# A tuned four-layer decoder trunk: the RMSNorm's per-token scale is spread over the partitions by two passes of ones on diagonal tiles in place of four, and later in the FFN

## The chip, the cores and the metric

The kernel runs on one core of a Trainium2 chip, as one program. The metric is the device time of one execution in microseconds (us). The engines are TensorE (PE, the matmuls, with a queue of its own for weight loads, PEld), VectorE (DVE), ScalarE (ACT), GpSimd (POOL) and SyncE (SP, which issues the weight transfers).

## What is computed

Four layers on 256 tokens of 1024 features. Each layer is a first gated feed-forward network (FFN), a token mixer, a second FFN, and a gated addition of an embedding (PLE). Every one of these four begins with an RMSNorm, so there are 16 norms.

```python
def rmsnorm(x, gain):
    xf = x.astype(jnp.float32)
    y = xf * lax.rsqrt(jnp.mean(xf * xf, axis=-1, keepdims=True) + EPS)
    return (y * gain.astype(jnp.float32)).astype(x.dtype)

def swiglu(x, w_gu, w_down):
    g, u = jnp.split(x @ w_gu, 2, axis=-1)
    return (jax.nn.silu(g) * u) @ w_down
# each layer:
#  h = x + 1/2 * SwiGLU_1(RMSNorm(x))
#  h = h + Mixer_{i mod 3}(RMSNorm(h))      (0 HGRN2, 1 mLSTM, 2 sliding window)
#  h = h + 1/2 * SwiGLU_2(RMSNorm(h))
#  x = h + sigmoid(RMSNorm(h) W_gate) * (p[i] W_ple)
```

## The kernel before, in words

All activations lie transposed: features on the 128 partitions, 256 tokens along the row. `h[0]` to `h[3]` hold the residual stream, each two feature tiles of 256 columns. Products are made to fp32 accuracy from fp32r parts: a number is split into a high and a low part, and three of the four partial products are summed.

**Weights** stream through in units of 1024 columns (`unit`, L225 is the transfer). Each unit is split: ACT casts the high part (`wh`, L250), DVE subtracts it from the raw weight (`wl`, L251). Six `wh` tiles and six `wl` tiles are in rotation, so a cast has to wait until PE has finished with the unit six before. `mm_t` then makes two matmuls for a 128x128 piece of weight: L282 (128x512: high weight with the high and the low part of x) and L283 (128x256: low weight with the high part of x). The first four columns of a product are made with the feature tile in the outer loop, so that a product can begin when the first x tile is there. L272 to L274 are the three matmuls of the form without folding.

**The norm is delayed.** The products do not wait for it: `push_tile` multiplies h by the gain only (L254 on ACT for the high part, L255 on DVE for the low part of an x tile, 128x256 each), and the product's result is multiplied by 1/rms afterwards. Meanwhile `norm_steps` makes 1/rms beside the product: squares, sums, a matmul with ones that gives each token's sum in a column (L416), a multiply-add (L390, DVE), a power of -0.5 (L391, POOL), which leaves `rc` with the tokens on the partitions. Then the spread turns `rc` into `rb`, where each partition holds all 256 values: for each half of the tokens a fp32 matmul of `rc` (broadcast along the row) with the identity (L421), which the chip runs as two passes each, four in all; ACT copies the result out (L423). These steps are background work of the product: `tick` counts units of weights, and a step is emitted when the weight of its predecessor (`yield W_RC`) has passed. The framework's scheduler then sets the final order on each engine, which runs its instructions in that order.

**Who reads rb.** In the FFN L442 (DVE) before the Silu; in HGRN L689. In PLE, `add`: the accumulators are folded (L311 on ACT, L312 on DVE) into `gs`, multiplied by rb (L544, DVE), a sigmoid follows (L545, ACT), two products (L546, L547, DVE) give the new h, and `push_tile` makes the next layer's x tiles from it. The next layer's first FFN product therefore begins behind PLE's whole chain.

**HGRN** multiplies gate slabs pairwise on DVE (L730, with the reciprocals L736 and L738) and makes the level matmuls L723 and, for the widest levels, L711 with `kc`, in two groups of four heads; PE has weight products in between. L808 scales the accumulators by rc.

Of the kernel before, what the change touches and what calls it, by code (L numbers as in the profile page):

```python
# [10 lines left out]
F32 = mybir.dt.float32  # L11
F32R = mybir.dt.float32r
# [6 lines left out]
P = 128  # L19
D = 1024  # L20
T = 256
NT = T // P
# [5 lines left out]
EPS = 1e-6  # L28
U = 1024
AHEAD_UNITS = 3  # L30
W_SQ, W_SS, W_RC = 1.0, 0.5, 0.5
ML_RATE = 1
SW_RATE = 2.5
FQ_RATE = 0.75
# [24 lines left out]
def weight_plan():  # L59
# [34 lines left out]
    for l, kind in enumerate(kinds()):  # L94
        j = (l // 3,)
        ffn(l, 0)
        if kind == 0:
            for hg in range(2):
                tiles("hg_w_in", j, run(D + hg * 512, 4) + run(hg * 512, 4), KT, 4)
            full("hg_w_in", j, 2 * D)  # L100
            for hf in range(2):
                pairs("hg_w_in", j, 3 * D + hf * 512, range(KT))
        elif kind == 1:
            tiles("ml_w_qkvo", j, run(0, 8), KT, 4)
            full("ml_w_qkvo", j, D)
            for hf in range(2):
                pairs("ml_w_qkvo", j, 2 * D + hf * 512, range(KT))
        else:
            pairs("sw_w_qkv", j, D, range(KT))
            for g in range(SW_H // SW_G):  # L110
                for k0 in (0, 4):
                    plan.append([("sw_w_qkv", j, k, [(g * 256, 256)]) for k in range(k0, k0 + 4)])
        full("w_ple_proj", (l,), 0, PLE // P)
        by_k(("hg_w_out", "ml_w_out", "sw_w_o")[kind], j)
        ffn(l, 1)
        tiles("w_ple_gate", (l,), run(0, KT), KT, 4)
# [3 lines left out]
class Kern:  # L120
# [30 lines left out]
    def small(self, shape, tag, bufs=2, dtype=F32):  # L151
        return self.tmp.tile(shape, dtype, tag=tag, name=self.nm(tag), bufs=bufs)

    def s512(self, name):
        return self.tmp.tile([P, 512], F32, tag="s512", name=self.nm(name), bufs=7)

    def pair(self):

# [190 lines left out]
    def setup(self):  # L349
        nc, c, a = self.nc, self.const, self.a  # L350
        self.h = [c.tile([P, 512], F32, tag=f"h{j}", name=f"h{j}") for j in range(4)]
        self.gains = c.tile([P, DEPTH * N_GAIN * KT], F32, name="gains")
        nc.scalar.dma_start(out=self.gains, in_=a["gains"])
        ncol = a["cols"].shape[1]
        self.cols = c.tile([P, ncol], F32, name="cols")
        self.ident = c.tile([P, P], F32, name="ident")
        make_identity(nc, self.ident)
        self.ones = c.tile([P, 1], F32, name="ones")
        nc.gpsimd.memset(self.ones, 1.0)
        self.mhalf = c.tile([P, 16], F32, name="mhalf")  # L360
        nc.gpsimd.memset(self.mhalf, -0.5)

# [27 lines left out]
        nc.vector.tensor_scalar(out=out, in0=src, scalar1=1.0 / n, scalar2=EPS, op0=ALU.mult, op1=ALU.add)  # L390
        nc.gpsimd.tensor_tensor(out=out, in0=out, in1=self.mhalf[:, :w], op=ALU.pow)  # L391

    def end_norm(self):


        rc = self.small([P, NT], "rc", 2)
        rb = self.small([P, T], "rb", 2)
        return self.x, rc, rb, self.later(self.norm_steps(rc, rb))

    def norm_steps(self, rc, rb):  # L400
        nc = self.nc
        ss = self.small([P, T], "ss", 2)
        for j in range(4):
            sq = self.s512("sq")
            nc.scalar.activation(sq, self.h[j], AF.Square)
            for i in range(2):
                s = sq[:, i * T:(i + 1) * T]
                if i:
                    nc.vector.tensor_tensor(out=ss, in0=ss if j else sq[:, :T], in1=s, op=ALU.add)
                elif j:  # L410
                    nc.vector.tensor_tensor(out=ss, in0=ss, in1=s, op=ALU.add)
            yield W_SQ
        yield W_SS
        ps = self.misc()
        for t in range(NT):
            nc.tensor.matmul(ps[:, t:t + 1], ss[:, t * P:(t + 1) * P], self.ones, start=True, stop=True)  # L416
        self.rsqrt_mean(rc, ps[:, :NT], D, NT)
        yield W_RC
        pb = self.misc()
        for t in range(NT):  # L420
            nc.tensor.matmul(pb[:, t * P:(t + 1) * P], rc[:, t:t + 1].broadcast_to([P, P]), self.ident,  # L421
                             start=True, stop=True)
        nc.scalar.copy(out=rb, in_=pb[:, :T])  # L423

    @staticmethod
# [7 lines left out]

    def ffn(self, l, f):
        nc = self.nc
        x, rc, rb, norm = self.end_norm()
        aT = [None] * FT
        todo = deque()

        def gate(j, g, u):  # L440

            nc.vector.tensor_tensor(out=self.two(g), in0=self.two(g), in1=self.bc(rb), op=ALU.mult)  # L442
            nc.scalar.activation(g, g, AF.Silu)  # L443
            nc.vector.tensor_tensor(out=g, in0=g, in1=u, op=ALU.mult)  # L444
            s = self.wide(F32R) if j >= 9 else self.slab(F32R)
            s4 = s.rearrange("p (c h t) -> p c h t", c=2, h=2)
            self.split(s4[:, :, 0, :], s4[:, :, 1, :], self.two(g))
            for i in range(2):
                aT[2 * j + i] = s[:, i * 512:(i + 1) * 512]

        def flush():
            while todo:
                gate(*todo.popleft())

        def gated(c, ps):
            if c % 2 == 0:
                return
            j = c // 4
            t = self.fold(ps, self.s512("gu"))
            if c % 4 == 1:  # L460
                self.g = t
                return
            todo.append((j, self.g, t))
            if len(todo) > 1:
                self.settle(norm)
            if norm not in self.bg:
                flush()

        self.gemm_tiles(x, 2 * FT, 4, gated)
        self.settle(norm)  # L470
        flush()
        self.start_norm(self.gain(l, 2 * f + 1))

        def added(c, ps):
            if c % 2 == 0:
                return
            j = c // 2
            y = self.fold(ps, self.s512("y"))
            nc.vector.tensor_tensor(out=self.two(y), in0=self.two(y), in1=self.bc(rb), op=ALU.mult)
            nc.vector.scalar_tensor_tensor(out=self.h[j], in0=y, scalar=0.5, in1=self.h[j],  # L480
                                           op0=ALU.mult, op1=ALU.add)
            self.push(j)

        self.gemm_tiles(aT, KT, 2, added)
# [800 lines left out]
```

## Time and profile before

| what | value |
|---|---|
| median of 3 runs | 2116.18 us (2113.44 to 2116.35) |
| the profiled execution's own time | 2116.68 us |
| its span in the trace | 2114.8 us |
| PE busy | 2087.5 us, 99% |
| PE weight loads busy | 1823.5 us, 86% |
| DVE busy | 1540.9 us, 73% |
| ACT busy | 1205.7 us, 57% |
| POOL busy | 52.9 us, 2% |

Busy times are sums over the whole execution. Matmuls are pipelined, so PE's busy time runs from a start to a modelled end; what a matmul costs PE is read from the distance between two starts. PE does not wait much, so the reader should look for the few places where it does.

### The profile page before, as it was taken

The page shows a single profiled execution, that of the slowest core. Times are in us where ns is not written, and L with a number is a line of the kernel's source. Part 1 is how long each engine was busy: PE and PEld are TensorE (multiplying, and loading weights), DVE is VectorE, ACT ScalarE, POOL GpSimd, SP SyncE. Part 2 cuts the span into 40 slices and gives each one's busy share as a digit, 9 for nine tenths or more (in the row PEclk, how much of TensorE's full clock was granted, in tenths as well). Part 3 has the DMA queues.
Part 4 walks back from the last instruction along what each step waited for, and adds up shares of the span by engine and source line. Part 5 has one row for each costly group of instructions (what it writes and reads, how often), then busy time and mean ns, then how long its engine had stood idle before and what let it go on. Part 6 is the DMA issues. An engine that isn't in the chain of part 4 may idle for free.

```text
span 2114.8 us, 30580 instructions
## 1 busy us (share of the span) xinstructions
PE 2087.5 (99%) x12269; PEld 1823.5 (86%) x12269; DVE 1540.9 (73%) x2065; ACT 1205.7 (57%) x1678; POOL 52.9 (2%) x84
## 2 busy tenths in 40 slices
PE   8999999999999999999999999999999999999998
PEld 7888889888888888888888888788888888898887
DVE  7766987776877576776687667777687768967766
ACT  6554656554755466655565557655465545565554
POOL 2000000000000000000000001000000000000000
PEclk9999999999999999999999999999999999999999
DMA  7555344555455544555555552355545453355552
GB/s 277 201 191 180 116 164 165 199 188 190 167 197 195 188 163 154 181 197 184 194 179 182 196 179 101 120 186 192 189 170 199 180 185 134 141 179 180 198 182 78
DMA packets 53999, 372.26 MB, mean 176 GB/s; under 512 B 6368, under 2 KB 7136, under 8 KB 9568
## 3 DMA queue, kind: packets, MB, share of 16 engines
q1 hardware_dynamic: 53712, 370.24, 48.8%
q8 instruction: 96, 1.57, 0.3%
q14 instruction: 47, 0.39, 0.1%
q10 hardware_dynamic: 144, 0.07, 0.0%
HBM read 369.23 MB, written 1.05 MB: 175 GB/s over the span
## 4 chain that ended last, share of the span: by engine, by line
PE 91%; DVE 4%; issue 2%; ACT 1%; POOL 1%; DMA 0%; SPq 0%; DVEq 0%; ACTq 0%; POOLq 0%
PE acc L282 50%; PE acc L283 25%; PE acc L272 2%; PE acc L274 2%; PE acc L273 2%; PE acc L264 2%; PE acc L263 2%; PE acc L265 2%; PE mis L723 1%; DVE wl L251 1%; DVE slab L730 1%; PE mis L1106 1%; DVE slab L736 1%; POOL rc L391 0%; PE mis L421 0%
## 5 line engine op out<-in xcount | busy, mean ns | idle before, releaser
L282 PE MATMUL acc<-x,wh 128*128 128x512 f32 x3384 | 1186.4, 395 | 6.0 <-ACT wh L250 5.9
L251 DVE TENSOR_TENSOR wl<-wraw,wh 128x1024 fp32r<-128x1024 f32 (+1 forms) x693 | 845.1, 1222 | 473.3 <-ACT wh L250 469.5
L250 ACT CAST wh<-wraw 128x1024 fp32r<-128x1024 f32 (+1 forms) x693 | 726.6, 1050 | 745.5 <-PE acc L282 434.6
L283 PE MATMUL acc<-x,wl 128*128 128x256 f32 x3384 | 947.3, 280 | 0.0
L282 PEld LDWEIGHTS acc<-x,wh 128*128 128x128 f32 x3384 | 635.8, 188 | 153.2 <-ACT wh L250 5.9
L283 PEld LDWEIGHTS acc<-x,wl 128*128 128x128 f32 x3384 | 639.1, 189 | 0.4 <-DVE wl L251 0.4
L282 PE MATMUL acc<-slab,wh 128*128 128x512 f32 x1152 | 403.8, 394 | 0.0
L283 PE MATMUL acc<-slab,wl 128*128 128x256 f32 x1152 | 321.5, 279 | 0.0
L282 PEld LDWEIGHTS acc<-slab,wh 128*128 128x128 f32 x1152 | 215.9, 187 | 50.0
L283 PEld LDWEIGHTS acc<-slab,wl 128*128 128x128 f32 x1152 | 217.2, 189 | 0.0
L312 DVE TENSOR_TENSOR gu<-acc,gu 128x512 f32<-128x512 f32 x176 | 120.4, 684 | 7.5 <-ACT gu L311 6.9
L311 ACT COPY gu<-acc 128x512 f32<-128x512 f32 x176 | 102.0, 580 | 16.9 <-PE acc L283 16.8
L272 PE MATMUL acc<-wh,x 128*128 128x512 f32 (+1 forms) x272 | 103.1, 380 | 0.0
L273 PE MATMUL acc<-wl,x 128*128 128x512 f32 (+1 forms) x272 | 100.8, 371 | 0.0
L274 PE MATMUL acc<-wh,x 128*128 128x512 f32 (+1 forms) x272 | 100.7, 370 | 0.0
L282 PE MATMUL acc<-wide,wh 128*128 128x512 f32 x256 | 91.7, 394 | 0.0
L263 PE MATMUL acc<-slab,wh 128*128 128x256 f32 x256 | 74.1, 291 | 0.1
L264 PE MATMUL acc<-slab,wh 128*128 128x256 f32 x256 | 72.9, 285 | 0.0
L265 PE MATMUL acc<-slab,wl 128*128 128x256 f32 x256 | 72.6, 284 | 0.0
L283 PE MATMUL acc<-wide,wl 128*128 128x256 f32 x256 | 71.4, 279 | 0.0
L254 ACT ACTIVATE x<-h,gains 128x256 fp32r<-128x256 f32 x128 | 57.5, 502 | 20.4 <-DVE h L480 19.9
L444 DVE TENSOR_TENSOR gu<-gu,gu 128x512 f32<-128x512 f32 x88 | 60.8, 692 | 6.0 <-ACT gu L443 2.9
(246 smaller groups left out, 1791.8 us busy)
## 6 DMA issues: line engine op xcount, KB each, us to landing
wraw<-in_w_all SPq DMA_DIRECT2D x346, 1024.0 KB, 4.8
wraw<-in_w_all SPq DMA_DIRECT2D x7, 512.0 KB, 7.8
pt<-in_pT SPq DMA_DIRECT2D x4, 256.0 KB, 4.1
h<-in_xT SPq DMA_DIRECT2D x3, 256.0 KB, 6.2
outT<-h SPq DMA_DIRECT2D x3, 256.0 KB, 2.0
wraw<-in_w_all SPq DMA_DIRECT2D x2, 256.0 KB, 4.5
h<-in_xT SPq DMA_DIRECT2D x2, 128.0 KB, 3.2
outT<-h SPq DMA_DIRECT2D x1, 128.0 KB, 1.7
```

The source lines that it names most:

```text
L250: self.nc.scalar.copy(out=hi, in_=src)
L251: self.nc.vector.tensor_tensor(out=lo, in0=src, in1=hi.bitcast(F32), op=ALU.subtract)
L263: mm(ps, wh[:, cs], xh, start=first and opens, stop=False, skip_group_check=True)
L264: mm(ps, wh[:, cs], xl, start=False, stop=False, skip_group_check=True)
L265: mm(ps, wl[:, cs], xh, start=False, stop=last, skip_group_check=True)
L272: mm(ps, xh[:, ts], wh[:, cs], start=first, stop=False, skip_group_check=True)
L273: mm(ps, xh[:, ts], wl[:, cs], start=False, stop=False, skip_group_check=True)
L274: mm(ps, xl[:, ts], wh[:, cs], start=False, stop=last, skip_group_check=True)
L282: mm(ps, wh[:, cs], x, start=first, stop=False, skip_group_check=True)
L283: mm(ps[:, T:], wl[:, cs], x[:, :T], start=False, stop=last, skip_group_check=True)
L311: nc.scalar.copy(out=o3, in_=p4[:, :, 1, :])
L312: nc.vector.tensor_tensor(out=o3, in0=p4[:, :, 0, :], in1=o3, op=ALU.add)
```

## The change

Three edits. A constant `ones_r` of 128x128 ones in fp32r is added. Behind `rc`, `split_scaled` makes two diagonal tiles of 128x128 for each of the high and the low part (identity times rc), which is two ACT (L254) and two DVE (L255) instructions of 128x128 per norm; the spread is then two fp32r passes of 128x256, ones times the high diagonals and ones times the low ones. And the FFN norms wait for 1.25 units in place of 0.5 between rc and the spread.

```diff
-W_SQ, W_SS, W_RC = 1.0, 0.5, 0.5
+W_SQ, W_SS, W_RC, W_RC_FFN = 1.0, 0.5, 0.5, 1.25
...
-    def s512(self, name):
-        return self.tmp.tile([P, 512], F32, tag="s512", name=self.nm(name), bufs=7)
+    def s512(self, name, dtype=F32):
+        return self.tmp.tile([P, 512], dtype, tag="s512", name=self.nm(name), bufs=7)
...
+        self.ones_r = c.tile([P, P], F32R, name="ones_r")
+        nc.scalar.copy(out=self.ones_r, in_=self.ones.broadcast_to([P, P]))
...
-    def end_norm(self):
+    def end_norm(self, w_rc=W_RC):
...
-        return self.x, rc, rb, self.later(self.norm_steps(rc, rb))
-
-    def norm_steps(self, rc, rb):
+        return self.x, rc, rb, self.later(self.norm_steps(rc, rb, w_rc))
+
+    def norm_steps(self, rc, rb, w_rc):
...
         self.rsqrt_mean(rc, ps[:, :NT], D, NT)
-        yield W_RC
+
+        d = self.s512("diag", F32R)
+        dh, dl = d[:, :T], d[:, T:]
+        for t in range(NT):
+            ts = slice(t * P, (t + 1) * P)
+            self.split_scaled(dh[:, ts], dl[:, ts], self.ident, rc[:, t:t + 1])
+        yield w_rc
         pb = self.misc()
-        for t in range(NT):
-            nc.tensor.matmul(pb[:, t * P:(t + 1) * P], rc[:, t:t + 1].broadcast_to([P, P]), self.ident,
-                             start=True, stop=True)
+        for i, d in enumerate((dh, dl)):
+            nc.tensor.matmul(pb[:, :T], self.ones_r, d, start=i == 0, stop=i == 1)
         nc.scalar.copy(out=rb, in_=pb[:, :T])
...
     def ffn(self, l, f):
         nc = self.nc
-        x, rc, rb, norm = self.end_norm()
+        x, rc, rb, norm = self.end_norm(W_RC_FFN)
```

From `end_norm` on the lines of the changed kernel stand some 7 further down: L421 and L423 become L429 and L430, L545 becomes L552, L723 becomes L730. The edits also move instructions that they do not touch, as the scheduler orders anew. Three places follow; numbers behind a name are the program's own and differ between the two kernels.

ACT in the PLE of layer 0, from the spread to the first x tiles of layer 1's FFN (x_4978 before, x_5000 in the change). Before:

```order
L250 CAST wh_5024<-wraw_5022 128x1024
L423 COPY rb_4810<-mis_4953 128x256
L545 ACT_TABLE_LOAD
L545 ACTIVATE gs_4909<-gs_4909 128x512
L311 COPY gs_4971<-acc_4923 128x512
L545 ACTIVATE gs_4916<-gs_4916 128x512
L250 CAST wh_5058<-wraw_5022 128x1024
L250 CAST wh_5086<-wraw_5084 128x1024
L254 ACTIVATE x_4978<-h_82,gains 128x256 x2
```

The change, at the same place (wh_5080 is the unit that was wh_5058, wh_5108 that which was wh_5086; acc_5027 is PLE's last accumulator):

```order
L254 ACTIVATE diag_4956<-ident,rc_4826 128x128 x2
L250 CAST wh_5080<-wraw_5044 128x1024
L430 COPY rb_4827<-mis_4975 128x256
L311 COPY gs_4993<-acc_4940 128x512
L250 CAST wh_5108<-wraw_5106 128x1024
L552 ACT_TABLE_LOAD
L552 ACTIVATE gs_4926<-gs_4926 128x512
L552 ACTIVATE gs_4933<-gs_4933 128x512
L552 ACTIVATE gs_4993<-gs_4993 128x512
L311 COPY gs_5066<-acc_5027 128x512
L250 CAST wh_5132<-wraw_5106 128x1024
L254 ACTIVATE x_5000<-h_82,gains 128x256 x2
```

The rb copy now has a cast ahead of it, and all three sigmoids, two folding copies and two casts stand between it and the first x tile, where a table load, two sigmoids, one copy and two casts stood.

PE in the first FFN product of layer 1, where the spread stands. Before, with the reduction L416 ahead of it:

```order
L416 MATMUL mis_5181<-ones,ss_5065 128x1 x2
L283 MATMUL acc_5170<-x_4987,wl_5111 128x256
L282 MATMUL acc_5170<-x_4996,wh_5110 128x512
L283 MATMUL acc_5170<-x_4996,wl_5111 128x256
L282 MATMUL acc_5170<-x_4996,wh_5110 128x512
L283 MATMUL acc_5170<-x_4996,wl_5111 128x256
L421 MATMUL mis_5200<-ident,rc_5056 128x128 x2
L282 MATMUL acc_5170<-x_5051,wh_5110 128x512
```

The change, the end of the same accumulator (its reduction stands 20 matmuls ahead of the first pass):

```order
L282 MATMUL acc_5192<-x_5073,wh_5132 128x512
L283 MATMUL acc_5192<-x_5073,wl_5133 128x256
L429 MATMUL mis_5239<-diag_5208,ones_r 128x256
L282 MATMUL acc_5192<-x_5073,wh_5132 128x512
L283 MATMUL acc_5192<-x_5073,wl_5133 128x256
L429 MATMUL mis_5239<-diag_5208,ones_r 128x256
L282 MATMUL acc_5252<-x_5000,wh_5158 128x512
```

The spread has moved from 5 matmuls behind the reduction to 20, and a pair of product matmuls stands between its two passes.

PE in the HGRN mixer of layer 0, second group of heads, at the first level matmul (L723; L730 in the change). Before:

```order
L274 MATMUL acc_2365<-wh_2427,x_1708 128x512
L272 MATMUL acc_2365<-wh_2427,x_1708 128x512
L273 MATMUL acc_2365<-wl_2428,x_1708 128x512
L274 MATMUL acc_2365<-wh_2427,x_1708 128x512
L723 MATMUL mis_2415<-slab_2068,slab_2350 128x128 x4
L723 MATMUL mis_2421<-slab_2068,slab_2350 128x128 x4
```

The change (wh_2439 is the unit that was wh_2427):

```order
L274 MATMUL acc_2377<-wh_2402,x_1715 128x512
L272 MATMUL acc_2376<-wh_2439,x_1715 128x512
L272 MATMUL acc_2377<-wh_2439,x_1715 128x512
L272 MATMUL acc_2615<-wh_2528,x_1463 128x512
L730 MATMUL mis_2427<-slab_2080,slab_2362 128x128 x4
L730 MATMUL mis_2433<-slab_2080,slab_2362 128x128 x4
```

The level matmuls stood behind all twelve matmuls of that unit and now stand behind two of them and one of a later unit.

## Rows read from the trace of the kernel before

**Rows 1.** The page: span, busy times, chain by engine, one group of weight loads.

```profile
span 2114.8 us, 30580 instructions
PE 2087.5 (99%) x12269; PEld 1823.5 (86%) x12269; DVE 1540.9 (73%) x2065; ACT 1205.7 (57%) x1678; POOL 52.9 (2%) x84
...
PE 91%; DVE 4%; issue 2%; ACT 1%; POOL 1%; DMA 0%; SPq 0%; DVEq 0%; ACTq 0%; POOLq 0%
...
L282 PEld LDWEIGHTS acc<-x,wh 128*128 128x128 f32 x3384 | 635.8, 188 | 153.2 <-ACT wh L250 5.9
```

**Rows 2.** One line, L421: durations in ns, idle before it.

```profile
L421 PE MATMUL mis<-ident,rc x64: 270/275/376, 41.9 to 2100.2; 128*128 128x128 f32 x64
...
  POOL rc L391: 12.0, 18
```

**Rows 3.** Timeline, layer 1's first FFN product: start us, us, instruction, idle before.

```profile
571.30 1.61 POOL L391 TENSOR_TENSOR rc<-rc,mhalf 128x2 f32<-128x2 f32 x1 [24.54 <-DVE rc L390]
...
571.60 0.28 PE L283 MATMUL acc<-x,wl 128*128 128x256 f32 x1
...
572.96 0.71 PE L421 MATMUL mis<-ident,rc 128*128 128x128 f32 x4 [1.08 <-POOL rc L391]
...
573.43 0.47 PE L282 MATMUL acc<-x,wh 128*128 128x512 f32 x1
```

**Rows 4.** PE's timeline, layer 0's PLE: the spread, and the last and first products.

```profile
546.81 0.71 PE L421 MATMUL mis<-ident,rc 128*128 128x128 f32 x4
547.28 0.36 PE L283 MATMUL acc<-x,wl 128*128 128x256 f32 x1
...
554.77 0.40 PE L282 MATMUL acc<-x,wh 128*128 128x512 f32 x1
555.01 0.28 PE L283 MATMUL acc<-x,wl 128*128 128x256 f32 x1
555.12 0.39 PE L282 MATMUL acc<-x,wh 128*128 128x512 f32 x1
```

**Rows 5.** ACT's timeline in the same stretch.

```profile
546.16 1.05 ACT L250 CAST wh<-wraw 128x1024 fp32r<-128x1024 f32 x1 [1.69 <-issue]
547.56 0.37 ACT L423 COPY rb<-mis 128x256 f32<-128x256 f32 x1 [0.35 <-PE mis L421]
547.95 1.28 ACT L545 ACT_TABLE_LOAD   x1
549.25 0.63 ACT L545 ACTIVATE gs<-gs 128x512 f32<-128x512 f32 x1
549.83 0.59 ACT L311 COPY gs<-acc 128x512 f32<-128x512 f32 x1
...
552.48 1.05 ACT L250 CAST wh<-wraw 128x1024 fp32r<-128x1024 f32 x1 [0.59 <-ACT wh L250]
553.43 0.91 ACT L254 ACTIVATE x<-h,gains 128x256 fp32r<-128x256 f32 x2
```

**Rows 6.** DVE's timeline in the same stretch.

```profile
553.97 0.89 DVE L255 SCALAR_TENSOR_TENSOR x<-h,gains,x 128x256 fp32r<-128x256 f32 x2 [0.36 <-ACT x L254]
```

**Rows 7.** Windows: stretch, length, busy time of the engines, granted clock (PEclk), DMA.

```profile
229.10:234.30 5.20, 3.77 (x28) 3.31 (x27) 5.20 (x9) 0.79 (x1) 0.00 (x0) 1.00 0.00 0
1266.20:1268.40 2.20, 0.00 (x0) 0.00 (x0) 1.02 (x3) 1.03 (x3) 0.47 (x1) 1.00 0.00 0
1268.40:1271.80 3.40, 3.40 (x16) 3.40 (x17) 1.52 (x2) 3.40 (x8) 0.00 (x0) 0.50 0.17 19
```

**Rows 8.** Timeline of PE and DVE in the HGRN mixer of layer 0.

```profile
230.92 0.46 PE L723 MATMUL mis<-slab,slab 128*128 128x128 f32 x2 [1.43 <-DVE slab L730]
...
253.70 0.49 PE L711 MATMUL mis<-slab,kc 128*128 128x128 f32 x2 [0.46 <-ACT kc L708]
...
264.21 3.35 DVE L736 RECIPROCAL slab<-slab 128x512 f32<-128x512 f32 x1
...
272.87 1.35 PE L723 MATMUL mis<-slab,slab 128*128 128x128 f32 x10 [0.95 <-DVE slab L730]
```

## The prediction

> **What bounds the kernel now.** I read the page first: busy times, then the chain that ended last. TensorE (PE) is busy 2087.5 of 2114.8 us and holds 91% of the chain; ScalarE (ACT) and VectorE (DVE) have 57% and 73% [rows 1]. So an edit pays only where PE waits or in PE's own passes, and it costs only where an engine with slack in the mean has none in one place. PE's pace comes from its timeline: in the PLE product a wide matmul takes its slot for .24 us and a narrow one for .11 us, start to start (554.77, 555.01, 555.12) [rows 4]; I use .35 us for the pair and .117 for the narrow one. Whatever a stretch takes above that pace is loss.
>
> Next came the line that is edited. The old spread has 64 passes, four for each of 16 norms, and the profile puts 12.0 us of idle time in front of them down to POOL's power (18 times, since PE's matmul and weight-load sequencers are both counted) [rows 2]. The timeline shows that this idle time is uneven. In a PLE norm the four passes take the place of one narrow slot for .47 us (546.81 to 547.28) and nothing waits long [rows 4]. In the first FFN half of layers 1 to 3, POOL's power takes 1.61 us and PE stands: the last narrow matmul starts at 571.60, its slot ends at 571.72, and the next product starts at 573.43, so 1.71 us are lost [rows 3]. Then I read ACT's and DVE's timelines from the PLE spread to the first product of the next FFN, since the PLE result, through ACT and DVE, is the only place where the spread feeds PE directly [rows 5, 6].
>
> **The change, part by part.**
>
> *Fewer passes.* 16 norms, two passes fewer each: .47 us becomes two narrow slots, .23 us, so .24 us each where nothing waits. The new pass is 128x256 in fp32r, as the narrow product is, and I price it like that one (.117); the bound above is the .18 us that an old pass takes when four take .71 [rows 4], which would add .06 x 32 = 2 us.
>
> *The diagonal tiles.* Each norm gains two ACT and two DVE instructions of 128x128. Not in the trace; on ACT between half of a 128x256 scaled copy and a whole one (.23 to .46, from .91 for two [rows 5]), and I take .35, so .70 for two, since part of a short instruction does not shrink with its size; on DVE between half of a 128x256 scale-and-subtract and a whole one (.22 to .45, from .89 for two [rows 6]), and I take .3. On engines with 43% and 27% idle that is nothing in the mean, and it is priced below where something queues behind it.
>
> *Later spread in the FFN.* In layers 1 to 3, first half, the spread moves from 5 matmuls (.9 us) behind the reduction to 20 (3.5 us). 1.61 us of power and the diagonal tiles (.7 and .3) fit in that, with .9 left for the reduction and the multiply-add. The 1.71 us fall to the passes' .23 and some .15 of splitting: -1.3 x 3 = **-3.9**. The four second halves had no long wait: -.25 x 4 = **-1.0**. What reads rb in the FFN (L442, behind the fold that frees the accumulator) is needed by the down product alone, far later; a late rb costs nothing there.
>
> *The PLE handover, where the cost is.* The PLE's delay weight is unchanged, yet the printed order of ACT moves there, in layers 0, 1 and 2 alike. Before: cast, rb copy, table load, sigmoid, copy, sigmoid, two casts, first new x tile. After: diagonal tiles, a cast, rb copy, a copy, a cast, table load, three sigmoids, a copy, a cast, first x tile. I walk the new queue through the old times of layer 0. Cast at 546.16, done at 547.2; diagonal tiles to 547.9. The next cast (wh_5080) writes the tile that wh_4880 held; two PLE weight units still follow that one on PE, 2 x 8 pairs x .35 = 5.6 us, and PLE ends at about 554.9 (555.12 before, less the .24 of the passes), so the tile is free at 549.3 and the cast ends at 550.3. That ACT does wait for a PE-held tile at such a cast is seen: .59 us before 552.48 [rows 5]. The rb copy ends at 550.6 where it ended at 547.93 [rows 5]. Then: gs copy to 551.2; cast wh_5108 waits for the tile of the last unit but one, free at 552.1, and ends at 553.2; table load 1.28, to 554.45; three sigmoids at some .56 each, to 556.15; the copy of the last accumulator, to 556.65; one cast, to 557.6; x high part .46, to 558.1; x low part on DVE .45 to .5, to 558.6. The first FFN product starts at 558.65 where it started at 555.12: **+3.5 us**, PE idle for 3.7.
>
> How firm is that? Suppose no cast waits for a tile. The last accumulator copy and the cast behind it still stand ahead of x in ACT's order, and that copy needs PLE's last matmul (ends about 555.2): copy .55, cast 1.0, x .46 and .45 give 557.7, a start 2.6 us later than now. That much follows from the order of the queue alone.
>
> Idle time has a second price. Before 1268.40 (sliding-window mixer) PE has 2.2 us with no matmul, and the 3.40 us behind it run at a granted clock of .50, 1.2 GHz in place of 2.4; a 1.43-us wait before 230.92 leaves it at 1.00 [rows 7, 8]. Its 16 matmuls take .21 us each there [rows 7]; those of 128x256 have the narrow slot of .117 at full clock, so the half clock cost 16 x .095 = 1.5 us. The new idle is longer than the one that was followed by half clock. So 5.0 x 3 = **+15.0**.
>
> *HGRN levels (layers 0 and 3).* In PE's order the first head group's level matmuls stand about 4 us later, so the wait of 1.43 us shrinks by .45 and the .46 us for kc goes [rows 8]; the spread saves .2. The second group's stand ten matmuls (.227 each) earlier, and with these 1.1 us PE reaches them at about 268.4. Their operands come from the reciprocal and its products on DVE, 272.87 less the 1.4 us by which one weight subtract fewer lets the 3.35-us reciprocal of 264.21 start earlier: 271.5. A wait of 3.1 us in place of .95 [rows 8]: +2.1. The two DVE diagonal instructions ahead of this chain add .6. Sum +1.6 x 2 = **+3.2**; bounds 0 (operands come as much earlier as the matmuls) and +3.3 each (half clock after the wait).
>
> *The other norms.* HGRN's passes are counted. First norm -.1; HGRN's remaining pass saving -.4; mLSTM +.25, since the diagonal tiles lengthen its chain and its order stays; sliding window -1.5, as the spread's new place covers most of the 2.2-us wait and so its half clock, of which I count half; last PLE +.6, as rb is late by the diagonal tiles on a tail that ACT and DVE set. Together **-1.15**.
>
> Sum: 15.0 - 3.9 - 1.0 + 3.2 - 1.15 = +12.15 us. The profiled execution took 2116.68 us (span 2114.8), which gives 2128.8; it stands .5 above the median of 2116.18, so against the median **2128.3 us**, +0.57%.
>
> A rule speaks against the passes too. Rows: in the product, slots of .24 and .11 us hold although each matmul has a weight load of 188 ns beside it [rows 1, 4], so the load is hidden. The Trainium skill, "TensorE: Matmul & The Clock Gate", section "Part 3: Packing small matmuls — row/col tiling", says that a load overlaps matmuls in flight only if its row group differs. By that rule each new pass would pay its load. The trace disagrees, as the slots show.
>
> **Rivals.**
> 1. *Handover without half clock.* For it: the 1.43-us wait kept the clock [rows 7]; against: the idle here is over twice that, and half clock followed the 2.2-us one. 10.5 in place of 15.0: 2123.8 us.
> 2. *HGRN at half clock after its longer waits.* For it: 3.1 us of idle is more than the 2.2 us; against: the operands' 1.4 us have a clear source in DVE's order. +1.7 per mixer,: 2131.7 us.
> 3. *Loads not hidden in the new passes.* 32 passes of .188 us [rows 1] = +6.0: 2134.3 us. Against: the slots above. The rule of the Trainium skill just named would have it so.
> 4. *The handover is hidden.* Place: ACT between the rb copy and the first x tile, before 555.12. For it: before, PE has no wait there, and x's first tile was ready at 554.46 (DVE's pair from 553.97 [rows 6]), .66 us early. Price: the 15.0 go, so 2116.18 - 2.85 = 2113.3 us, no measurable change with HGRN as above. It ends on the faster side if HGRN's term is also under .9 us per mixer: with it at 0 the sum is -6.05, 2110.1 us. It decides if the first x tile is no more than .66 us later than now. Against: the 2.6-us floor.
>
> **How the numbers follow.** I call 0.2% (4.2 us) what a measurement here can tell from no change: 2112.0 to 2120.4. Forecast .50; rival 1 .23; rival 2 .09; rival 3 .02; rival 4 with HGRN as reckoned .10, with HGRN at nothing .06. So faster .06, same .10, slower .84. The range 2119.5 to 2133.5 runs from below rival 1 (its 2.6-us floor, 10.5 less 2.7, and HGRN less 1.6: 2119.5) to past rival 2, and leaves out rival 4 and rival 3, .18.
>
> **What would show it.** The handover: PE idle 3 to 4 us in front of the first FFN product of layers 1 to 3 with ACT's x tile or DVE's behind it as releaser, rb copy ending near 550.6, then a stretch at .50 clock. The FFN spread: no PE wait in front of the new passes, and passes of .117. HGRN: PE waits longer in front of the second group's first level matmul and less in front of the first's. The prediction is wrong if PE enters the FFN without a wait, or if the spread's wait comes back in front of the new passes.

## The result and the profile after

The changed kernel took 2143.53 us, median of 4 runs (2139.17 to 2148.87), against 2116.26 for the kernel before: a ratio of 1.0135, 95% interval 1.0116 to 1.0154, 27.3 us slower. Two further measurements of it gave 1.0163 (1.0140 to 1.0186) and 1.0157 (1.0134 to 1.0180). The direction was as forecast; 2143.5 lies 10 us above the range's upper end of 2133.5. The profiled execution took 2139.17 us.

The page after answers to [rows 1]: the span is 22.7 us longer, and a new releaser stands in the costliest PE group, DVE's low part of the x tiles.

```profile
span 2137.5 us, 30587 instructions
PE 2097.6 (98%) x12237; PEld 1829.2 (86%) x12237; DVE 1547.5 (72%) x2097; ACT 1215.4 (57%) x1711; POOL 50.7 (2%) x84
...
PE 93%; DVE 3%; ACT 2%; issue 1%; POOL 0%; DMA 0%; SPq 0%; POOLq 0%; DVEq 0%; ACTq 0%
...
L282 PE MATMUL acc<-x,wh 128*128 128x512 f32 x3384 | 1195.3, 397 | 17.1 <-DVE x L255 11.5
```

PE's timeline at the handover from layer 0's PLE to layer 1's FFN answers to [rows 4], where the last product was followed by the first with no wait.

```profile
553.33 0.28 PE L283 MATMUL acc<-x,wl 128*128 128x256 f32 x1
557.43 0.77 PE L282 MATMUL acc<-x,wh 128*128 128x512 f32 x1 [3.81 <-DVE x L255]
557.99 0.41 PE L283 MATMUL acc<-x,wl 128*128 128x256 f32 x1
558.21 0.63 PE L282 MATMUL acc<-x,wh 128*128 128x512 f32 x1
...
558.85 0.63 PE L282 MATMUL acc<-x,wh 128*128 128x512 f32 x1
```

The profile puts 3.81 us of idle down to the x tile; between the starts there are 3.98 us above the pace. Then a pair takes .64 us (558.21 to 558.85) instead of .35. The windows of the same place show why: behind the five engines' busy times stands the granted clock, .50 for the 5.25 us behind the idle stretch, then back.

```profile
553.30:557.43 4.13, 0.32 (x3) 0.03 (x1) 4.04 (x8) 4.13 (x9) 0.00 (x0) 0.84 0.22 91
557.43:562.68 5.25, 5.25 (x16) 4.47 (x17) 5.25 (x11) 3.49 (x7) 0.00 (x0) 0.50 0.00 0
562.68:567.93 5.25, 5.25 (x31) 4.61 (x31) 5.24 (x10) 3.54 (x5) 0.00 (x0) 0.97 0.54 200
```

ACT's timeline there answers to [rows 5]:

```profile
545.75 0.69 ACT L254 ACTIVATE diag<-ident,rc 128x128 fp32r<-128x128 f32 x2
547.85 1.05 ACT L250 CAST wh<-wraw 128x1024 fp32r<-128x1024 f32 x1 [1.41 <-PE acc L282]
548.80 0.37 ACT L430 COPY rb<-mis 128x256 f32<-128x256 f32 x1
549.07 0.59 ACT L311 COPY gs<-acc 128x512 f32<-128x512 f32 x1
550.76 1.05 ACT L250 CAST wh<-wraw 128x1024 fp32r<-128x1024 f32 x1 [1.10 <-PE acc L282]
551.83 1.28 ACT L552 ACT_TABLE_LOAD   x1
553.12 1.67 ACT L552 ACTIVATE gs<-gs 128x512 f32<-128x512 f32 x3
554.70 0.56 ACT L311 COPY gs<-acc 128x512 f32<-128x512 f32 x1
555.17 1.04 ACT L250 CAST wh<-wraw 128x1024 fp32r<-128x1024 f32 x1
556.12 1.70 ACT L254 ACTIVATE x<-h,gains 128x256 fp32r<-128x256 f32 x4
```

The queue is the one that was walked through ahead of the run, with both casts waiting for a tile that PE holds. To read it against the forecast, shift by 1.4 us: PLE ends at 553.45 here, where 554.9 was reckoned.

### The profile page after: what moved, and what is told of

Its sections match the earlier page's. It is cut to its first block, busy times and chain, and to the rows that moved or that the text cites. A ratio compares the mean times of both kernels' runs of the same rounds, so it can differ in the third digit from the quotient of the medians.

```text
span 2137.5 us, 30587 instructions
## 1 busy us (share of the span) xinstructions
PE 2097.6 (98%) x12237; PEld 1829.2 (86%) x12237; DVE 1547.5 (72%) x2097; ACT 1215.4 (57%) x1711; POOL 50.7 (2%) x84
## 4 chain that ended last, share of the span: by engine, by line
PE 93%; DVE 3%; ACT 2%; issue 1%; POOL 0%; DMA 0%; SPq 0%; POOLq 0%; DVEq 0%; ACTq 0%
PE acc L282 51%; PE acc L283 26%; PE acc L274 2%; PE acc L273 2%; PE acc L272 2%; PE acc L264 2%; PE acc L263 2%; PE acc L265 2%; PE mis L730 1%; PE mis L1113 1%; DVE wl L251 1%; DVE slab L737 1%; ACT wh L250 1%; PE mis L718 0%; PE mis L429 0%
## 5 line engine op out<-in xcount | busy, mean ns | idle before, releaser
L254 ACT ACTIVATE x<-h,gains 128x256 fp32r<-128x256 f32 x128 | 57.1, 501 | 23.7 <-DVE h L487 19.1
```

## A second thing in the traces: two pitches of the product

The waits and the half clock do not make up the whole difference. Two windows of 100 us in the long stretches of two FFNs of this one trace (nothing but product matmuls, no idle time, granted clock 1.00):

```profile
1640.00:1740.00 100.00, 100.00 (x579) 87.43 (x578) 67.97 (x76) 52.89 (x66) 0.00 (x0) 1.00 0.53 190
1980.00:2080.00 100.00, 100.00 (x568) 86.73 (x567) 67.60 (x76) 52.43 (x65) 0.00 (x0) 1.00 0.52 190
```

579 matmuls in one, 568 in the other, for the same work. Between starts, a pair takes 346.7 ns on average in the first and 353.3 in the second (350, 350, 360 in turn): the short and the long pitch below (the expectations call the long one the slow pace). A whole stretch holds one pitch; a change comes only where something else stands between the products, such as a norm's spread or a mixer. In each trace I cut the pairs into blocks of 24, and summed 24 times what the mean pitch of a block has above 346.7 ns. That is what the long pitch cost: 8.0 us in the profiled execution of before, 11.9 in that of the change. The span less that sum is called the time at equal pitch: 2106.8 and 2125.6 us, a difference of 18.8. The kernels' executions spread over 10 us and more, so medians of 4 to 12 executions carry some us of this, and I read each experiment by both numbers.

One more thing varies. The mixer of layer 2 (sliding window) holds a stretch at half clock whose length differs from trace to trace, from none to 13.65 us. From the last product pair of layer 2's first FFN to the first of its second, the seven traces that have the old spread in that mixer's norm (before and e1, e2, e4, e8, e9, e10 below) take 106.2 to 110.7 us; the eight with the new one take 106.8 to 112.9. The wait of 2.25 us that [rows 7] show there is followed by half clock within 1.4 us in before, e1 and e8, and by none in e2, e9 and e10. The time at equal pitch still holds this.

## The experiments

Theory A, from the prediction: the change costs what ACT's new order at the three PLE handovers costs. Rivals: B, each new spread costs its share, 27.3 / 16 = 1.7 us; C, the later spread in the FFN costs. Two more came up with the first results: D, the later or new spread in the FFN lets the long pitch through; E, the pitch is drawn by chance, whatever the kernel. The diffs show the lines that decide; the parameters that they pass on are left out.

**The later spread alone** (e1), with the old passes:

```diff
-        x, rc, rb, norm = self.end_norm()
+        x, rc, rb, norm = self.end_norm(W_RC_FFN)
```

> Edit: the FFN norms wait 1.25 units, the old four passes everywhere. Theory A (the cost of the change is ACT's new order at the PLE handover, which the diagonal tiles of the PLE norms bring): no diagonal tiles, so the handovers are as before, and PE's 1.71 us of loss at the spread of layers 1 to 3 shrink to the passes' .5, -1.2 x 3 = -3.6: 2112 to 2114 us. Theory B (the new spread costs its share at each of the 16 norms, 27.3 / 16 = 1.7 us): no new spread, so also 2112 to 2116. Theory C (the later spread in the FFN is what costs): 20 us or more above before, 2136 to 2144.

Measured: 2121.40 us, ratio 1.0020 (1.0004 to 1.0036), where I expected a gain. C's 20 us are not there, but neither is the gain in the time. In the trace .90 us above the pace are left in front of the passes in each of the three places (1.25 before): the old spread moves only from 5 to 7 matmuls behind the reduction there, not to 20 as in the changed kernel. At equal pitch the trace is at 2104.7, 2.1 below before, and the long pitch cost 11.3 us against 8.0. This miss led to D.

**The new spread in the PLE norms alone** (e2):

```diff
     def ple(self, l):
-        x, rc, rb, norm = self.end_norm()
+        x, rc, rb, norm = self.end_norm(new=True)
```

(`new` picks the spread; it is False in all other norms, and the FFN waits 0.5 units.)

> Edit: the new spread in the four PLE norms alone, all else as before, no later spread. Theory A: each of the three handovers has PE idle for 3.98 us and a stretch at half clock behind it; counted between like matmuls of the two traces the three took 6.6, 6.6 and 5.6 us, 18.8 in all, and the last PLE norm .7: 2134 to 2137 us, 71% of the whole change. Theory B: four norms of 16, 4 x 1.7 = 6.8 us: 2123. Theory C: 2116.

Measured: 2124.76 us, ratio 1.0035 (1.0019 to 1.0051). By its median this is B's number. The trace says otherwise. At the first handover, PE:

```profile
551.19 0.28 PE L283 MATMUL acc<-x,wl 128*128 128x256 f32 x1
555.24 0.77 PE L282 MATMUL acc<-x,wh 128*128 128x512 f32 x1 [3.77 <-DVE x L255]
```

The three handovers take 6.6, 6.6 and 6.7 us more than before, counted between like matmuls of the two traces, 19.9 in all: A's mechanism, from four norms alone. The median is low for two other reasons in the main. The waits at the next FFN's spread (1.25 above the pace, three times) are gone, since that spread, itself unchanged, now stands 9 matmuls behind the reduction and not 5; and the long pitch cost 2.4 us in place of 8.0. At equal pitch it is 2120.9, 14.1 above before.

**The changed kernel with the old passes in the PLE norms** (e3), all others new:

```diff
     def ple(self, l):
-        x, rc, rb, norm = self.end_norm()
+        x, rc, rb, norm = self.end_norm(new=False)
```

> Edit: the changed kernel with the old four passes in the four PLE norms alone. Theory A: the three handovers are as before, 0.0 us of wait in front of the first FFN product; the change loses 18.8 + .7: 2143.5 - 19.5 = 2124 us by the medians, and by the sum of the other terms in the two traces (FFN spreads -4.8, HGRN +3.9, first norm +1.0, sliding window +.7) 2117: so 2115 to 2125. Theory B: 2143.5 - 6.8 = 2137. Theory C: 2143.

Measured: 2121.61 us, ratio 1.0037 (1.0017 to 1.0057), 22 us less than the change; no wait at any handover. That is A's number, not B's 2137 or C's 2143. At equal pitch 2110.7. One thing came back: with the handovers hidden, each first FFN half of layers 1 to 3 waits 1.2 us at its new spread, since the diagonal tiles wait for a power that takes 1.52 us again. What the change gained in the FFN hung on the idle time that it made at the handover.

**The new spread in HGRN alone** (e4):

```diff
     def hgrn(self, l):
-        x, rc, rb, norm = self.end_norm()
+        x, rc, rb, norm = self.end_norm(new=True)
```

(As in e2, `new` is False in all other norms, and the FFN waits 0.5 units.)

> Edit: the new spread in the two HGRN norms alone, all else as before. The prediction's term: first head group's level wait 1.15 us in place of 1.59 above the pace, second group's 3.27 in place of 1.11, sum +1.6 to +2.0 per mixer: 2119.5 to 2120.5 us. Theory B: 2 x 1.7 = 3.4: 2119.7, but spread evenly, with the waits in front of the level matmuls as before. If HGRN's shift in the changed kernel came from something else than its own norm (the FFN's later spread ahead of it): 2116.

Measured: 2121.58 us, ratio 1.0025 (1.0009 to 1.0041). The rows are those forecast. PE, layer 0, the first and the second group of heads (L736 and L743 are this kernel's L723 and L730), to be set beside [rows 8]:

```profile
229.81 1.46 PE L736 MATMUL mis<-slab,slab 128*128 128x128 f32 x11 [1.00 <-DVE slab L743]
...
267.28 0.91 PE L736 MATMUL mis<-slab,slab 128*128 128x128 f32 x6 [3.13 <-DVE slab L743]
```

1.00 in place of 1.43, and 3.13 in place of .95. HGRN's shift comes from its own diagonal tiles. Between like matmuls the mixer of layer 0 takes 1.9 us more than before and that of layer 3 takes 1.2; in this trace half clock (3.41 us) follows the longer wait in layer 0 alone. The trace is 6.2 us above before at equal pitch, and 3.6 of these lie in layer 2's mixer, which this edit leaves alone and which stands at half clock for 10.24 us here, 3.41 before.

**The change once more** (e5).

> Edit: none, the changed kernel once more, since a second thing shows in the traces: in whole stretches of 100 to 300 us a pair of product matmuls takes 353.3 ns instead of 346.7 (three pairs of 350, 350, 360), at a granted clock of 1.00; 8.0 us of the profiled execution of before and 11.9 us of the changed one. If which stretches are slow is drawn anew in each execution, the executions spread over some 10 us, 2136 to 2150, median near 2125.6 (the changed trace's 2137.5 less 11.9) + 1.9 + 8 to 12 = 2136 to 2140, and the slow stretches of the new trace are others. If they belong to the kernel, median 2140 to 2145 and the same stretches. The three handovers take 6.6, 6.6 and 5.6 us again in both cases.

Measured: 2148.06 us (2141.70 to 2153.48); the trace has handovers of 5.7, 6.8 and 5.7 us, the long pitch in other stretches than the first trace, at a cost of 13.0 us, and 2127.4 at equal pitch. So the stretches are drawn anew, yet the median lies above the 2136 to 2140 that E gave.

**Matmuls that fill the handover** (e6):

```diff
         self.gemm_tiles(x, KT, 4, gated, (KT - 1,) if last else ())
+        if not last:
+            pd = self.misc()
+            for i in range(14):
+                nc.tensor.matmul(pd, self.ones_r, x[i % 8], start=i == 0, stop=i == 13)
         self.settle(norm)
```

> Edit: the changed kernel with 14 matmuls of 128x512 more (ones times PLE's x tiles, a result that nothing reads) between PLE's last product and the first FFN product of the next layer. They fill 14 x .23 = 3.2 of the 3.98 us that PE waits there. If the half clock behind each wait is the price of PE's idle time, it goes: -2.6, -2.6 and -1.5 us, 6.7 below the changed kernel; the first FFN product starts no later than before and its first pairs take .35 us, not .64. If the half clock has another cause, no change. If the x tiles are late for another reason than ACT's queue (PE's own work in front), the handover gets longer by up to 3.2 us each, +9.6.

Measured: 2140.01 us, ratio 1.0125 (1.0108 to 1.0142), 8.0 below e5 on the same chip. PE at the first handover:

```profile
558.80 3.43 PE L587 MATMUL mis<-x,ones_r 128*128 128x512 f32 x14
562.70 0.50 PE L282 MATMUL acc<-x,wh 128*128 128x512 f32 x1 [0.47 <-DVE x L255]
...
563.15 0.39 PE L282 MATMUL acc<-x,wh 128*128 128x512 f32 x1
```

The x tile is as late as before, and the second pair behind it starts .45 us after the first, where a half-clock pair took .64; all later ones take .35. The handovers cost 4.1 us each in place of 5.6 to 6.8. So some 1.5 to 2.7 us of each were the half clock, and PE's idle time brings it. At equal pitch 2122.6, 4.8 below e5.

**The high part of the diagonal tiles on DVE** (e7), which takes the tiles out of ACT's queue and leaves all else:

```diff
-            self.split_scaled(dh[:, ts], dl[:, ts], self.ident, rc[:, t:t + 1])
+            nc.vector.tensor_scalar(out=dh[:, ts], in0=self.ident, scalar1=rc[:, t:t + 1], scalar2=None, op0=ALU.mult)
+            nc.vector.scalar_tensor_tensor(out=dl[:, ts], in0=self.ident, scalar=rc[:, t:t + 1],
+                                           in1=dh[:, ts].bitcast(F32), op0=ALU.mult, op1=ALU.subtract)
```

> Edit: the changed kernel with the high part of the diagonal tiles made by VectorE in place of ScalarE; passes, VectorE's low part and the later spread stay. ACT's order in PLE is then: rb copy, cast, copy, table load, three sigmoids, cast, first x tiles, and the copy of the last accumulator and a further cast come behind x. Theory A (ACT's order at the handover): by the old times cast to 547.2, rb by 548.5, cast 549.3 to 550.3, copy 550.9, table 552.1, sigmoids 553.8, cast 554.8, x 555.3 and 555.8, PLE's end at 554.9: .9 us of wait and no half clock, in place of 3.98 us and 2.3: 18.8 - 2.7 = 16 us less than the changed kernel, 2124 to 2128. Theory B (the new passes and tiles cost everywhere): no gain, 2140 to 2145.

Measured: 2126.35 us, ratio 1.0067 (1.0045 to 1.0088), 22 us below e5. ACT's timeline at the first handover:

```profile
546.45 1.05 ACT L250 CAST wh<-wraw 128x1024 fp32r<-128x1024 f32 x1 [1.09 <-PE acc L282]
547.40 0.58 ACT L311 COPY gs<-acc 128x512 f32<-128x512 f32 x1
548.00 1.28 ACT L554 ACT_TABLE_LOAD   x1
549.30 1.68 ACT L554 ACTIVATE gs<-gs 128x512 f32<-128x512 f32 x3
550.88 1.04 ACT L250 CAST wh<-wraw 128x1024 fp32r<-128x1024 f32 x1
551.93 1.71 ACT L254 ACTIVATE x<-h,gains 128x256 fp32r<-128x256 f32 x4
553.54 0.56 ACT L311 COPY gs<-acc 128x512 f32<-128x512 f32 x1
```

The copy of the last accumulator now stands behind x, and the handover costs 1.8 to 1.9 us, with no half clock behind it. The passes are the same 32. This is a strong run for A: the price hangs on two small ACT instructions, through the order that they bring. Not all of the 22 us is the handover, though. Of the 21.3 us between the spans of the two traces, 12.4 to 12.7 lie in the three handovers, some 5 in HGRN, where the second group's wait is back at .97 us and no half clock follows, and 3.1 in the pitch.

**The old spread, later by 2.25 units in the FFN** (e8): one number, 23 matmuls behind the reduction in the first halves of layers 1 to 3, 36 in the second halves.

```diff
-W_SQ, W_SS, W_RC = 1.0, 0.5, 0.5
+W_SQ, W_SS, W_RC, W_RC_FFN = 1.0, 0.5, 0.5, 2.25
```

> Edit: the kernel before with one number changed: the FFN norms wait 2.25 units between rc and the old four passes, so that these stand 23 matmuls behind the reduction in the first halves of layers 1 to 3 (5 before, 7 with 1.25 units, where .90 us of wait above the pace were left). The 1.71 us of loss shrink to the passes' .47: -1.24 x 3 = -3.7, and no diagonal tiles: 2112.9 us, the version that should beat both kernels. If POOL's power, which takes 1.6 us there, moves along with DVE's subtracts, some of the wait stays: 2114 to 2116.

Measured: 2117.51 us, ratio 1.0020 (1.0009 to 1.0032), a miss by its median. The trace has what was meant to come: no wait in front of those spreads, 2101.7 at equal pitch, 5.1 below before. The long pitch took 11.4 us of it back.

**Only the first halves later** (e9) and **only the second halves later** (e10), old passes:

```diff
-        x, rc, rb, norm = self.end_norm(W_RC_FFN)
+        x, rc, rb, norm = self.end_norm(W_RC if f else W_RC_FFN)     # e9
+        x, rc, rb, norm = self.end_norm(W_RC_FFN if f else W_RC)     # e10
```

> Edit: the kernel before with the old spread, 2.25 units late in the first FFN halves of layers 0 to 3 only. The last call showed that the long FFN stretch behind a spread (508 to 522 pairs, 3.4 us more if slow) was fast in all 12 second halves of the three kernels that have the old position there, and slow in 11 of 28 where the spread is later. Theory D (the later spread itself lets the slow pace through in the second halves): with those left alone, the gain of the first halves comes out whole: 3.7 us below before. Theory E (which stretches are slow is drawn by chance, whatever the kernel): also 3.7 below before. If the later spread is no gain in the first halves: the same as before.

> Edit: the kernel before with the old spread, 2.25 units late in the second FFN halves only. At the pace of 346.7 ns nothing is gained or lost there (no wait before, none after): within 1 us of before. Theory D: slow stretches in 40% of the four second halves, 4 x .4 x 3.4 = 5.4 us above before. Theory E: within 1.5 us of before.

Measured: e9 2105.85 us, ratio 0.9966 (0.9953 to 0.9980), faster than both kernels by more than was expected; e10 2118.69 us, ratio 1.0018 (1.0002 to 1.0035), 4.7 us slower by the medians. No long wait is at stake there: the old passes cost .70 us above the pace in each second half of before, and .45 where they stand later. e9's trace has the short pitch in the long stretches of all eight FFNs (the long pitch cost 1.7 us in all) and 2102.4 at equal pitch. Of its seven executions five lie within .41 us (2105.45 to 2105.86) and two stand 3.5 and 3.9 us above their median; one long stretch costs about 3.4. e10's has the long one in three, two of them second halves (12.4 us in all, 2104.5 at equal pitch). That is nearer D's 5.4 for e10 than E's 1.5, but the interval, .4 to 7.4 us, holds D's number and reaches E's.

**The new spread, not later** (e11): the changed kernel with W_RC_FFN = 0.5.

> Edit: the changed kernel with all norms at 0.5 units, so that the new spread stands 16 matmuls behind the reduction in the FFN, not 20. The three handovers stay (18.8 us by the traces), HGRN's stays, and with 16 matmuls the FFN's wait stays hidden. Trace at equal pace: within 1.5 us of the changed kernel's. Theory A with E: median 2140 to 2148 as the changed kernel. Theory C (the later spread costs): 15 us or more below. Theory D: at most 5 us below.

Measured: 2141.10 us (2130.69 to 2147.87), ratio 1.0126 (1.0102 to 1.0150). As the changed kernel: handovers of 5.6 to 5.7 us, three of the four second halves long, 2129.2 at equal pitch. The number 1.25 plays next to no part in the loss.

**The changed kernel with the old spread in the four second halves** (e12), beside **the changed kernel** (e13):

```diff
-        x, rc, rb, norm = self.end_norm(W_RC_FFN)
+        x, rc, rb, norm = self.end_norm(*((W_RC, False) if f else (W_RC_FFN, True)))
```

> Edit: the changed kernel with the old four passes at 0.5 units in the four second FFN halves only. The three handovers, HGRN and the first halves stay, so at equal pace it is within 1.5 us of the changed kernel (a loss of at most 1 us for the passes). Theory D (the old spread, 9 matmuls behind the reduction, ends the slow pace; the new one lets it through): all four long stretches of the second halves run at 346.7 ns, and the median falls by 4 x .45 x 3.4 = 6 us against the changed kernel run beside it, 2137 to 2142. Theory E (chance, whatever the kernel): the same median as the changed kernel, within 3 us.

> Edit: none, the changed kernel on the same chip as the run before it. Theories A and D: 2140 to 2150 us, handovers of 3.9 us of wait, one to three of the four long stretches in the second halves slow.

Measured: 2136.81 us, ratio 1.0113 (1.0090 to 1.0136), and 2144.70, 7.9 apart where D said 6 and E at most 3; at equal pitch the two traces are .7 apart (2125.8 and 2126.5). Windows of e12 in its four second halves, and then of e13 in the last two (its first two have 579 matmuls as well):

```profile
380.00:480.00 100.00, 100.00 (x579) 87.43 (x578) 72.79 (x81) 56.13 (x73) 0.00 (x0) 1.00 0.53 190
900.00:1000.00 100.00, 100.00 (x579) 88.19 (x578) 70.22 (x78) 54.61 (x70) 0.00 (x0) 1.00 0.53 189
1400.00:1500.00 100.00, 100.00 (x579) 88.15 (x578) 71.65 (x80) 55.60 (x72) 0.00 (x0) 1.00 0.54 190
1980.00:2080.00 100.00, 100.00 (x579) 88.16 (x578) 69.40 (x78) 53.43 (x67) 0.00 (x0) 1.00 0.54 190
```

```profile
1400.00:1500.00 100.00, 100.00 (x569) 86.77 (x568) 71.51 (x81) 54.64 (x71) 0.00 (x0) 1.00 0.53 189
1980.00:2080.00 100.00, 100.00 (x568) 86.67 (x567) 67.60 (x74) 51.90 (x66) 0.00 (x0) 1.00 0.53 189
```

Over the 15 traces, the long stretches behind the spread of a second half:

| spread in the second halves | traces | with the long pitch |
|---|---|---|
| old passes, 9 matmuls behind the reduction | before, e2, e4, e9, e12 | 0 of 20 |
| old passes, 20 or 36 behind | e1, e8, e10 | 4 of 12 |
| new passes, tiles by ACT and DVE | the change, e3, e5, e6, e11, e13 | 14 of 24 |
| new passes, tiles by DVE | e7 | 0 of 4 |

The first halves have no such order: the long pitch stands in 17 of their 60 stretches, and in 5 of 12 where the old spread stands as before (before, e4, e10). D is borne out for the second halves alone.

## Why the forecast was too low

The direction and the mechanism of the handover were forecast rightly; the sum was not. The terms, with what they measure between like product matmuls of the two profiled executions, in us:

| term of the sum | forecast | measured |
|---|---|---|
| three handovers, with the fewer passes of their PLE norms | +15.0 | +17.9 |
| FFN spread, first halves of layers 1 to 3 | -3.9 | -4.6 |
| fewer passes in the four second halves | -1.0 | -1.0 |
| two HGRN mixers | +3.2 | +3.9 |
| other norms | -1.15 | +3.0 |
| pitch of the product | none | +3.9 |
| start of the first product | none | -.4 |
| sum | +12.15 | +22.7 |

(The forecast of the other norms holds -.4 for HGRN's passes; measured, these are in HGRN's row.)

Three steps failed. PE's pace was taken as one constant, .35 us a pair, so the pitch stood in the sum at nothing: +3.9. The other norms were sized -1.15: +3.0. And the half clock behind the handovers was priced at 1.5 us each: 2.6, 2.6 and 1.6. The third is the smallest in effect; the handovers' 2.9 us alone would have given 2131.2, within the range.

**The handover** was read rightly: its queue, its tiles, its idle time (3.98 us above the pace for 3.7 forecast), the half clock behind it. e3 and e7 show that it goes when the order goes, e2 that the PLE norms alone bring it. Its size was off: 6.6, 6.6 and 5.6 us between like matmuls, 18.8, less .9 for the passes of the PLE norms, which the forecast's 15.0 holds too. I took the price of the half clock from one stretch of 3.40 us in the sliding window, 16 narrow matmuls at .095. Here a pair at half clock takes .64 us, and eight pairs did so (5.25 us) at two handovers. The third paid 1.6 us, as all three do in e11 and e12: so the price was right for a short stretch, and how long the stretch lasts is what the forecast did not ask. Rival 1, no half clock, is refuted by the clock's rows; rival 4, the hidden handover, by the 3.98 us; rival 3 by passes of .12 us (below).

**HGRN** has the waits that were reckoned: second group 3.11 us in the changed kernel for 3.1 forecast, first group .99 for .98. Its sum, +1.9 and +2.0 us between like matmuls for +1.6 each, holds something else as well: rival 2 came about. PE in layer 0, and the window behind the second wait:

```profile
230.66 1.13 PE L730 MATMUL mis<-slab,slab 128*128 128x128 f32 x8 [0.99 <-DVE slab L737]
...
268.06 2.52 PE L730 MATMUL mis<-slab,slab 128*128 128x128 f32 x16 [3.11 <-DVE slab L737]
```

```profile
269.42:272.83 3.41, 3.41 (x12) 2.93 (x12) 3.25 (x5) 0.00 (x0) 0.00 (x0) 0.50 0.76 267
```

Layer 3 has 3.41 us at .50 behind its second wait too; before, neither mixer has any. Without half clock (e4, layer 3) the new spread costs 1.2 us, with 3.41 us of it 1.9 to 2.6, with 6.83 us (e5 and e12 in layer 3, e6 in layer 0) 3.1 to 3.3. So the waits cost less than forecast, the half clock made up for it, and that +1.6 is near +1.9 is in part luck.

**The FFN spread** gained 1.5 us in each first half for 1.3 forecast. The reason given, 1.25 units, is not what brings it: e11 has it with 0.5, and e3 has 1.25 and lacks it. The order does, and it follows PE's idle time at the handover.

**Fewer passes** gained what was forecast, .23 to .27 us in each second half and .3 in each of the three PLE norms, but by two errors that cancel. The old four passes were read as .47 us from their first start; PE waits in front of them. The second half of layer 0, before:

```profile
362.18 0.39 PE L282 MATMUL acc<-x,wh 128*128 128x512 f32 x1
362.56 0.71 PE L421 MATMUL mis<-ident,rc 128*128 128x128 f32 x4
...
363.22 0.40 PE L282 MATMUL acc<-x,wh 128*128 128x512 f32 x1
```

From one wide matmul to the next there are 1.04 us where the pace is .35: the spread costs .70. In the change, DVE, PE and its weight loads:

```profile
363.01 0.28 PE L283 MATMUL acc<-x,wl 128*128 128x256 f32 x1
363.06 0.61 DVE L255 SCALAR_TENSOR_TENSOR diag<-ident,rc,diag 128x128 fp32r<-128x128 f32 x2
363.13 0.28 PE L429 MATMUL mis<-diag,ones_r 128*128 128x256 f32 x1
363.25 0.39 PE L282 MATMUL acc<-x,wh 128*128 128x512 f32 x1
363.48 0.28 PE L283 MATMUL acc<-x,wl 128*128 128x256 f32 x1
363.72 0.19 PEld L429 LDWEIGHTS mis<-diag,ones_r 128*128 128x128 f32 x1 [0.28 <-DVE diag L255]
363.72 0.38 PE L429 MATMUL mis<-diag,ones_r 128*128 128x256 f32 x1
363.94 0.40 PE L282 MATMUL acc<-x,wh 128*128 128x512 f32 x1
```

The first pass takes the narrow slot (363.13 to 363.25), as priced. The second waits for the low part of the tiles, which DVE ends at 363.67, and its weight load waits with it: it starts .24 us behind a matmul whose slot is .12, and takes .22 itself. .12 + .12 + .22 = .46 us for both, not .23. The profile counts such waits for DVE nine times over both queues, and for ACT thirteen. Where nothing waits, the old four cost .44 to .45 (e1, e8 and e10 at the same places), and the new two .24, in e7:

```profile
361.43 0.40 PE L431 MATMUL mis<-diag,ones_r 128*128 128x256 f32 x2
361.67 0.40 PE L282 MATMUL acc<-x,wh 128*128 128x512 f32 x1
```

So the wait for DVE's low part, priced at nothing wherever no product queues behind it, took .22 of the .46 us that two passes could have saved here. The Trainium skill, "TensorE: Matmul & The Clock Gate", section "Part 3: Packing small matmuls — row/col tiling", has the rule on row groups by which every pass would pay its load (the section also names a background weight buffer); the first pass at .12 us, with a load of .19 us ahead of it, disagrees with that rule, and the second pays for a wait.

**The other norms** were sized -1.15 and came to +3.0: first norm +1.0 (its first pass waits 1.30 us for the diagonal tile), sliding window +1.2 for -1.5 (the wait for kd shrank to 1.02 us, but a wait of 1.33 came at another line, and the half clock stands behind that one instead), mLSTM +.25, last PLE +.6. The sliding window's number is that of these two traces, which both hold 3.41 us at half clock there; with the spread told above, one pair of traces does not settle it.

**What was not in the sum at all** is the pitch. The prediction took .35 us a pair as constant, and called all above it loss. In the profiled execution the long pitch cost 3.9 us more than before, and where it stands is drawn anew: in two first halves before, in three second halves in the change. The medians stand further apart than the spans' 22.7: 27.3, 35.5 and 32.0 us in the three measurements. How much of the rest is pitch and how much half clock is not shown, as only profiled executions have a trace. e12 gives 7.9 us back with the second halves restored, e10 loses 4.7 with these moved alone, and 0 of 20 against 18 of 40 stretches bear D out. What in the spread sets the pitch is not settled: e1 and e7 have no long second half although their spreads are later or new.

## What to carry to other kernels

A small instruction added to an engine that is idle two fifths of the time can cost through the order that a scheduler makes of it: walk the engine's new queue at the place where the bottleneck hands over, with the waits for tiles in it. Fewer matmul passes gain less than their slots where one waits for a tile of its own, since the weight load waits with it: .24 us here where .46 were to be had. Read the cost of a pass from the product matmul before it to the one behind it, not from its own start. And before a change of some us is priced, count the matmuls in equal windows of one trace and look for stretches at half clock: if either varies, a median moves with it. What did help was one number: the old spread 2.25 units later in the first FFN halves alone, 0.34% faster than the kernel before.

## What the runs showed that I had not expected

The product's two pitches, 346.7 and 353.3 ns a pair at a granted clock of 1.00, 579 and 568 matmuls in 100 us, held for some 180 us at a stretch. The half clock behind the same idle time of PE cost 1.6 or 2.6 us at like handovers, and behind the same 2.25 us in layer 2's mixer there was none in three traces. With 14 matmuls put into the idle time (e6) no handover had it. And POOL's power of 128x2 took .70 us in the changed kernel's FFN of layer 1, and 1.61 us [rows 3] where weight subtracts ran on DVE beside it.
